# Convolved feed-forward block: four up products from unscaled rows, the other forty from normalised rows, and a later embedding product

## The chip, the cores and the metric

The kernel runs on one core of a Trainium2 chip. The metric is the device time of one execution in microseconds, the median of several runs. The engines are TensorE (PE, with its weight loads shown as PEld), VectorE (DVE), ScalarE (ACT), GpSimd (POOL) and SyncE (SP, which here only issues transfers).

## The reference, cut to what matters

One layer of a streaming encoder over 2048 positions of 1024 channels, in float32:

```python
def rms_norm(x, g):
    return x * rsqrt(mean(x * x, -1) + 1e-6) * g

h = rms_norm(x, mix_norm_g);  z = h @ w_in                # 3328 columns
y = concat(short_conv_mixer(z[:, :1536]), rwkv7_mixer(z[:, 1536:]))
x = x + y @ w_out
# feed-forward: 5632 = 2 * 2816 columns
u = causal_dwconv(rms_norm(x, ffn_norm_g) @ ffn_w_up, conv_w) + conv_b   # width 3, per channel
gate, val = split(u, 2)
x = x + (silu(gate) * val) @ ffn_w_down
# per-layer embedding
e = rms_norm(p @ ple_w_proj, ple_norm_g)
x = x + sigmoid(rms_norm(x, ple_gate_norm_g) @ ple_w_gate) * e
out = rms_norm(x, final_norm_g)
```

`causal_dwconv` at position t reads positions t-2, t-1 and t of the same channel. `rwkv7_mixer` is a recurrence over the positions.

## The kernel before, in words

**Layout.** Channels lie on the 128 partitions, positions on the free axis. The positions are cut into four groups of G = 512, so one tile is 128 x 512 and a row of 1024 channels is KD = 8 tiles. Every dense product is made in three passes of a split format: a float32 tile is held as a rounded high part `hi` and a remainder `lo`, weights as `whi`, `wlo`, and `mm3` issues whi x hi, whi x lo and wlo x hi for each of the 8 tiles, in the order of the tiles: 24 matmuls for one output tile ("a product"). Products are written to a PSUM tile of tag `d`, of which there are three.

**Stages.** First the input projection of all four groups. Then, for each group, `dense_rest`: 8 out products (`whlo` in the trace), 44 up products (`whlu`), of which numbers i and 22 + i make pair i, down products (`whld`) after every fourth pair, the embedding products (`ple_embed`, `whlpj`), and 8 gate products (`whlg`). The recurrence of the time mixer (16 units) is a generator of small steps on the side; `drive` issues one step at about every half product, so its small matmuls stand between the large ones. It has ended before the fourth group's dense work begins.

**Order.** The matmuls keep the order in which the program issues them. On the other engines a planner orders instructions when the kernel is built: among those that are ready it takes the first in program order, with all that stands in a `high_priority` block ahead of the rest. A queue then runs in that fixed order, and the first instruction that waits holds all behind it. POOL also issues the loads of the split weights (line 161); in the first group it makes them (line 154).

**The rows and their scale.** After each out product the tile `x2[m]` is squared into a running sum, and split into `hi`, `lo` of x2 times the gain (line 214 on ACT, 215 on DVE), without the factor 1/rms of the position, which needs all 8 tiles. `product` therefore starts the up products from unscaled rows: the results of the first two (HELD = 2) are copied to SBUF (line 281), then `rstd` makes the factor by one matmul (`ps_norm`) and a chain of ACT and DVE instructions (lines 239 to 248). From then on the factor is applied in each evacuation: `scaled` multiplies the PSUM tile by it into a tile `zb` with two columns in front (line 255 on DVE), POOL copies the last two columns of the previous group in and the new ones out (lines 256 and 257), ACT makes `uf` = w2 * zb + bias (line 412), and DVE adds the two shifted terms (line 417, twice). For a pair, `act_pair` then makes silu(gate) * val (lines 429 to 433) and splits it (line 153 on ACT, 154 on POOL).

**Buffers.** `hi` and `lo` tiles share 32 slots (tag `act`), working tiles of tag `b` share 6, `zb` has 2.

Of the kernel before, what the change touches and what calls it, by code (L numbers as in the profile page):

```python
# [9 lines left out]
F32 = mybir.dt.float32  # L10
F32R = mybir.dt.float32r
AF = mybir.ActivationFunctionType
ALU = mybir.AluOpType
# [3 lines left out]
P = 128  # L17
G = 512
KD = 8
FIN = 1  # L20
PLE_AT = 2
HELD = 2
WAIT = 20
R_BONUS = 1
# [13 lines left out]
NFF = 22  # L38
# [24 lines left out]
def tile_trunk(  # L63
# [18 lines left out]
    nc = tc.nc  # L82
# [13 lines left out]
    cpool = ctx.enter_context(tc.tile_pool(name="cpool", bufs=1))  # L96
# [23 lines left out]
    def v(name, i, n=1):  # L120
        o, _ = VEC[name]
        return vec[:, o + i : o + i + n]
# [19 lines left out]
    z_last = cpool.tile([P, 14], F32, tag="z_last", name="z_last")  # L142
    cx_last = cpool.tile([P, 4, 2], F32, tag="cx_last", name="cx_last")
    u_last = cpool.tile([P, 44, 2], F32, tag="u_last", name="u_last")
    for t in (z_last, cx_last, u_last):
        nc.vector.memset(t, 0.0)

# [4 lines left out]
    def residual(raw, hi, lo):  # L152
        nc.scalar.copy(hi, raw)  # L153
        nc.gpsimd.tensor_tensor(out=lo, in0=raw, in1=hi.bitcast(F32), op=ALU.subtract)  # L154

    def half(pools, src, name, key):
        t = pools["w"].tile([P, 1024], F32R, tag="whl", name=f"whl{name}", bufs=WHL)
        hi, lo = t[:, 0:512], t[:, 512:1024]
        if key in kept:
            with tc.high_priority():  # L160
                nc.gpsimd.dma_start(out=t, in_=kept[key])  # L161
            return hi, lo
        first = pools["w"].tile([P, 512], F32, tag="raw", name=f"raw{name}", bufs=WRAW)
        with tc.high_priority():
            if len(src.shape) == 3:
                nc.sync.dma_start(out=first.rearrange("p (j c) -> p j c", j=2), in_=src)
            else:
                nc.sync.dma_start(out=first, in_=src)
            residual(first, hi, lo)
        keep = dram.tile([P, 1024], F32, tag=f"k{name}", name=f"k{name}")  # L170
        nc.sync.dma_start(out=keep, in_=t.bitcast(F32))
        kept[key] = keep
        return hi, lo
# [3 lines left out]
    def weight(pools, src, name):  # L177
        return [
            half(pools, src[:, 512 * c : 512 * c + 512], f"{name}_{c}", f"{name}_{c}")
            for c in range(2)  # L180
        ]
# [5 lines left out]
    def mm3(ps, w, k, h, start, stop):  # L187
        whi, wlo = w[k // 4]
        cols = blk(k % 4)
        hhi, hlo = h  # L190
        matmul(ps, whi[:, cols], hhi, start=start, stop=False)
        matmul(ps, whi[:, cols], hlo, start=False, stop=False)
        matmul(ps, wlo[:, cols], hhi, start=False, stop=stop)
# [4 lines left out]
    def buf(pools, name):  # L198
        return pools["tmp"].tile([P, G], F32, tag="b", name=name, bufs=NBUF)
# [6 lines left out]
    def slot(pools, name):  # L206
        return pools["act"].tile([P, G], F32R, tag="act", name=name)

    def pair(pools):
        return slot(pools, "hi"), slot(pools, "lo")  # L210
# [42 lines left out]
    def scaled(pools, ps, rstd, halo, pad):  # L253
        zb = pools["tmp"].tile([P, G + 2], F32, tag="zb", name="zb")
        nc.vector.tensor_tensor(out=zb[:, 2 : G + 2], in0=ps, in1=rstd, op=ALU.mult)  # L255
        nc.gpsimd.tensor_copy(zb[:, 2 - pad : 2], halo)
        nc.gpsimd.tensor_copy(halo, zb[:, G + 2 - pad : G + 2])
        return zb
# [10 lines left out]
    def product(pools, w, rows, evac):  # L269
        ps = pools["psd"].tile([P, G], F32, tag="d", name="ps_mm")  # L270
        for k in range(KD):
            mm3(ps, w, k, rows.hs[k], k == 0, k == KD - 1)
            if k == 3:
                yield
        if rows.ss is None or rows.scale is not None:
            with tc.high_priority():
                evac(ps, rows.scale)
        else:
            with tc.high_priority():
                raw = buf(pools, "raw")  # L280
                nc.scalar.copy(raw, ps)
            rows.held.append((raw, evac))
            if len(rows.held) == HELD:
                rows.scale = rows.ss.rstd(pools)
                with tc.high_priority():
                    for raw, evac in rows.held:
                        evac(raw, rows.scale)
        yield
# [59 lines left out]
    def ple_rows(pools, g):  # L348
        hs = []
        with tc.high_priority():  # L350
            for k in range(2):
                hi, lo = pair(pools)
                t = staged(pools, pT[k, :, g * G : (g + 1) * G], "p")
                residual(t, hi, lo)
                hs.append((hi, lo))
        return hs

    def ple_embed(pools, g, st):
        hs = st
        ss = SumSq()  # L360
        for mp in range(KD // 2):
            w = quad(pools, w_proj, mp, f"pj{mp}")
            for mm in range(2):
                m = 2 * mp + mm
                ps = pools["psd"].tile([P, G], F32, tag="d", name="ps_e")
                for k in range(2):
                    mm3(ps, w, 2 * k + mm, hs[k], k == 0, k == 1)
                with tc.high_priority():
                    t = buf(pools, "e")
                    nc.scalar.copy(t, ps)  # L370
                    nc.scalar.dma_start(out=es[g][:, m, :], in_=t)
                ss.add(pools, t)
            yield
        embed[g] = ss
# [12 lines left out]
    def dense_rest(pools, g, yrows, nxt):  # L387
        tmp = pools["tmp"]
        gs = slice(g * G, (g + 1) * G)
        x2 = []  # L390
        rows = Rows()
# [13 lines left out]
            if m == FIN and pending:  # L405
                pending.pop()()

        def up(n, st, key):
            def evac(ps, rstd):
                zb = scaled(pools, ps, rstd, u_last[:, n, :], 2)  # L410
                u = st[key] = buf(pools, "uf")
                nc.scalar.activation(  # L412
                    u, zb[:, 2 : G + 2], AF.Identity,
                    bias=v("ffn_conv_b", n), scale=v("ffn_conv_w", 88 + n),
                )
                for d in (1, 0):
                    nc.vector.scalar_tensor_tensor(  # L417
                        out=u, in0=zb[:, d : d + G], scalar=v("ffn_conv_w", 44 * d + n),
                        in1=u, op0=ALU.mult, op1=ALU.add,
                    )  # L420
            return product(pools, weight(pools, w_up[n], f"u{n}"), rows, evac)

        def act_pair(i, acts):
            st = {}
            yield from up(i, st, "g")
            yield from up(NFF + i, st, "v")
            with tc.high_priority():
                th = buf(pools, "th")
                nc.scalar.activation(th, st["g"], AF.Tanh, scale=0.5)
                nc.vector.scalar_tensor_tensor(  # L430
                    out=th, in0=th, scalar=1.0, in1=st["g"], op0=ALU.add, op1=ALU.mult
                )
                nc.vector.tensor_tensor(out=th, in0=th, in1=st["v"], op=ALU.mult)
                hi, lo = pair(pools)
                residual(th, hi, lo)
                acts.append((hi, lo))
# [3 lines left out]
        def down(first, acts, last=False):  # L440
            n = len(acts) // 2
            for mp in range(KD // 2):
# [18 lines left out]
                        yield  # L461
                yield

        prev = None
        for first in range(0, NFF, NB):
            acts = []
            for i in range(first, min(first + NB, NFF)):
                if i == first + 2 and prev is not None:
                    yield from down(first - NB, prev)
                yield from act_pair(i, acts)  # L470
                if i == PLE_AT - 1:
                    prows = ple_rows(pools, g)
                if i == PLE_AT:
                    yield from ple_embed(pools, g, prows)
                if i == PLE_AT + 1:
                    embed[g] = embed[g].rstd(pools)
# [7 lines left out]
        for m in range(KD):  # L484
            nxt(m)
            w = weight(pools, w_gate[m], f"g{m}")
# [4 lines left out]
            def evac(ps, rstd, m=m, e=e):  # L491
                th = buf(pools, "gt")
                nc.vector.tensor_tensor(out=th, in0=ps, in1=rstd, op=ALU.mult)
                if m:
                    ss.add(pools, x2[m - 1])
                nc.scalar.activation(th, th, AF.Tanh, scale=0.5)
                nc.vector.scalar_tensor_tensor(
                    out=th, in0=th, scalar=1.0, in1=e, op0=ALU.add, op1=ALU.mult
                )
                nc.vector.scalar_tensor_tensor(  # L500
                    out=x2[m], in0=th, scalar=pg_h[:, m : m + 1], in1=x2[m],
                    op0=ALU.mult, op1=ALU.add,
                )
                if m == KD - 1:
                    ss.add(pools, x2[m])
# [428 lines left out]
    pools, rp = {}, {}  # L934
# [24 lines left out]
    rows = {(kind, g): Rows() for kind in ("in", "out") for g in range(NG)}  # L959
# [114 lines left out]
```

## Time and profile before

| what | value |
|---|---|
| median of 3 runs | 2914.36 us (2904.48 to 2923.4) |
| the profiled execution's own time | 2908.45 us |
| its span, first to last instruction | 2906.5 us |
| mean granted clock of TensorE | 0.984 of full speed |
| busy: PE, DVE, POOL, ACT | 95%, 66%, 38%, 33% of the span |

A stretch of the trace is given in microseconds from the start of the span. The up products of the four groups run at 747 to 1230, 1350 to 1804, 1912 to 2366 and 2465 to 2840, with the down and embedding products among them. Consecutive matmuls overlap in the record, so their spacing, not their mean duration, tells the rate.

### The profile page before, as it was taken

How to read it: one execution, taken by the hardware profiler on the slowest of the kernel's cores; microseconds unless marked ns; L12 is line 12 of the kernel's file. 1: busy time of each engine (PE TensorE's matmuls, PEld its weight loads, DVE VectorE, ACT ScalarE, POOL GpSimd, SP SyncE). 2: the span in 40 equal slices, each digit the busy share in tenths (PEclk: the TensorE clock that was granted, in tenths of full speed). 3: DMA queues.
4: the chain of work that ended last, by engine and by line, in shares of the span. 5: the costliest groups of instructions: out<-in, count | busy, mean ns of one | idle time of the engine just before them, and what ended most of it. 6: DMA issues, size and time to landing. Idle time of an engine off the chain costs nothing.

```text
span 2906.5 us, 42153 instructions
## 1 busy us (share of the span) xinstructions
PE 2768.1 (95%) x15464; PEld 2226.7 (77%) x15464; DVE 1908.3 (66%) x3039; ACT 959.9 (33%) x1721; POOL 1117.4 (38%) x1700
## 2 busy tenths in 40 slices
PE   8999999999889999989999999999999999999997
PEld 5778888778677877767778887777788877788885
DVE  5575665648587868796766676857676765544446
ACT  5332232312553433443412223434222143411113
POOL 4533232324556565652333333333333332433221
PEclk9999999999999999989999999999999999999998
DMA  8887777767777777767666565766565668666665
GB/s 298 297 261 217 236 214 223 209 210 243 263 252 245 258 241 247 248 228 230 178 186 185 173 192 172 233 202 200 174 192 169 187 187 266 216 195 189 196 188 169
DMA packets 285802, 629.95 MB, mean 217 GB/s; under 512 B 60186, under 2 KB 113690, under 8 KB 285596
## 3 DMA queue, kind: packets, MB, share of 16 engines
q0 software_dynamic: 95040, 346.07, 39.4%
q1 hardware_dynamic: 134144, 232.83, 24.0%
q10 hardware_dynamic: 56412, 48.36, 5.2%
q8 instruction: 122, 2.00, 0.3%
q14 instruction: 84, 0.69, 0.1%
HBM read 467.77 MB, written 159.38 MB: 216 GB/s over the span
## 4 chain that ended last, share of the span: by engine, by line
PE 50%; DVE 22%; DMA 14%; issue 6%; ACT 5%; POOL 3%; ACTq 1%; SPq 0%; DVEq 0%; POOLq 0%
PE ps_mm L86 33%; PE ps_d L86 11%; DVE uf L417 3%; DVE pd L794 3%; DVE xs L798 2%; DMA lm<-ld 1%; DMA xd<-xs 1%; DMA ld<-ltt 1%; DVE zb L255 1%; DVE sq L229 1%; DMA es<-e 1%; PE o_ps L86 1%; DMA dt<-xd 1%; DVE lo L215 1%; DMA x<-in_xT 1%
## 5 line engine op out<-in xcount | busy, mean ns | idle before, releaser
L86 PE MATMUL ps_mm<-hi,whlu 128*128 128x512 f32 x2816 | 910.6, 397 | 11.3 <-POOL whlu L154 5.1
L86 PEld LDWEIGHTS ps_mm<-hi,whlu 128*128 128x128 f32 x2816 | 532.3, 189 | 131.9 <-POOL whlu L154 7.8
L86 PE MATMUL ps_mm<-hi,whlin 128*128 128x512 f32 x1664 | 542.9, 400 | 19.6 <-ACT whlin L153 7.1
L86 PE MATMUL ps_mm<-lo,whlu 128*128 128x512 f32 x1408 | 552.3, 392 | 1.5 <-DVE lo L215 1.5
L86 PE MATMUL ps_d<-hi,whld 128*128 128x512 f32 x1408 | 456.1, 396 | 16.7 <-DMA whld<-kd 7.2
L86 PEld LDWEIGHTS ps_mm<-hi,whlin 128*128 128x128 f32 x1664 | 316.7, 190 | 93.0 <-ACT whlin L153 7.1
L417 DVE SCALAR_TENSOR_TENSOR uf<-zb,vec,uf 128x512 f32<-128x512 f32 x352 | 298.6, 851 | 89.6 <-ACT uf L412 78.4
L86 PE MATMUL ps_mm<-lo,whlin 128*128 128x512 f32 x832 | 328.9, 395 | 2.8 <-DVE lo L215 2.8
L412 ACT ACTIVATE uf<-zb,vec 128x512 f32<-128x512 f32 x176 | 143.1, 815 | 562.0 <-DVE zb L255 536.8
L86 PEld LDWEIGHTS ps_d<-hi,whld 128*128 128x128 f32 x1408 | 265.6, 189 | 79.2 <-DVE x L457 8.4
L86 PEld LDWEIGHTS ps_mm<-lo,whlu 128*128 128x128 f32 x1408 | 266.8, 189 | 56.2 <-DVE lo L215 2.4
L161 POOL DMA_DIRECT2D whlu<-ku x264 | 141.7, 537 | 436.8 <-PE ps_mm L86 289.1
L255 DVE TENSOR_TENSOR zb<-ps_mm,rstd 128x512 f32<-128x512 f32 x216 | 148.5, 688 | 208.0 <-PE ps_mm L86 204.4
L86 PE MATMUL ps_d<-lo,whld 128*128 128x512 f32 x704 | 275.4, 391 | 0.0
L457 DVE TENSOR_TENSOR x<-ps_d,x 128x512 f32<-128x512 f32 x192 | 131.6, 687 | 139.5 <-PE ps_d L86 138.7
L86 PEld LDWEIGHTS ps_mm<-lo,whlin 128*128 128x128 f32 x832 | 158.4, 190 | 38.1 <-DVE lo L215 6.6
L161 POOL DMA_DIRECT2D whlin<-kin x156 | 84.1, 539 | 248.9 <-PE ps_mm L86 207.7
L86 PE MATMUL ps_mm<-hi,whlg 128*128 128x512 f32 x512 | 169.2, 406 | 3.4 <-DMA whlg<-kg 3.4
L86 PE MATMUL ps_mm<-hi,whlo 128*128 128x512 f32 x512 | 163.1, 397 | 8.5 <-DMA whlo<-ko 4.9
L154 POOL TENSOR_TENSOR lo<-th,hi 128x512 fp32r<-128x512 f32 x88 | 115.2, 1310 | 110.9 <-ACT hi L153 110.3
L154 POOL TENSOR_TENSOR whlu<-rawu,whlu 128x512 fp32r<-128x512 f32 x88 | 122.6, 1398 | 88.9 <-ACT whlu L153 79.2
L86 PEld LDWEIGHTS ps_d<-lo,whld 128*128 128x128 f32 x704 | 133.2, 189 | 26.0
(205 smaller groups left out, 4248.0 us busy)
## 6 DMA issues: line engine op xcount, KB each, us to landing
whlu<-ku POOLq DMA_DIRECT2D x264, 512.0 KB, 4.5
whlin<-kin POOLq DMA_DIRECT2D x156, 512.0 KB, 4.8
whld<-kd POOLq DMA_DIRECT2D x132, 512.0 KB, 4.0
ku<-whlu SPq DMA_DIRECT2D x88, 512.0 KB, 4.7
kin<-whlin SPq DMA_DIRECT2D x52, 512.0 KB, 5.3
whlo<-ko POOLq DMA_DIRECT2D x48, 512.0 KB, 5.5
whlg<-kg POOLq DMA_DIRECT2D x48, 512.0 KB, 3.9
rawu<-in_w_up SPq DMA_DIRECT2D x88, 256.0 KB, 4.1
```

Source lines behind the costliest of these rows:

```text
L86: return pin(nc.tensor.matmul(*args, **kw))
L154: nc.gpsimd.tensor_tensor(out=lo, in0=raw, in1=hi.bitcast(F32), op=ALU.subtract)
L161: nc.gpsimd.dma_start(out=t, in_=kept[key])
L215: nc.vector.scalar_tensor_tensor(out=lo, in0=src, scalar=gcol, in1=hi.bitcast(F32), op0=ALU.mult, op1=ALU.subtract)
L229: nc.vector.tensor_tensor(out=sq, in0=sq, in1=self.acc, op=ALU.add)
L255: nc.vector.tensor_tensor(out=zb[:, 2 : G + 2], in0=ps, in1=rstd, op=ALU.mult)
L412: nc.scalar.activation(u, zb[:, 2 : G + 2], AF.Identity, bias=v("ffn_conv_b", n), scale=v("ffn_conv_w", 88 + n),)
L417: nc.vector.scalar_tensor_tensor(out=u, in0=zb[:, d : d + G], scalar=v("ffn_conv_w", 44 * d + n), in1=u, op0=ALU.mult, op1=ALU.add,)
L457: nc.vector.tensor_tensor(out=x2[m], in0=ps, in1=x2[m], op=ALU.add)
L794: tt(out=pd[:, :, :, 0:n], in0=xs[:, :, None, 0:n].broadcast_to([P, 8, 2, n]), in1=lm[:, None, i : i + 2, 0:n].broadcast_to([P, 8, 2, n]), ...
L798: nc.vector.tensor_reduce(out=xs[:, :, i : i + 2], in_=pd[:, :, :, 0:n], op=ALU.add, axis=mybir.AxisListType.X,)
```

## The change

The first four up products of a group (pairs 0 and 1) are computed and evacuated as before. While they run, `norm_rows` makes the eight rows anew with the factor applied, as a second set of `hi`, `lo`: three rows after pair 0's second product, three after pair 1's first, two after its second. The other 40 products take these rows, so that their PSUM tile is already scaled: ACT and DVE read it directly, without `zb`. The two columns that reach back into the previous group are made once for all 44 products (`halos`) and added to the first two columns. ACT, not POOL, keeps the last two columns. The embedding's rows, products and factor move back by two pairs (`PLE_AT` from 2 to 4).

```diff
-PLE_AT = 2
+PLE_AT = 4
+RAW_UP = 2
...
+    halo = cpool.tile([P, 44, 2], F32, tag="halo", name="halo")
...
+        nrows = Rows()
+        nrows.ss = None
+
+        def halos():
+            w0, w1 = v("ffn_conv_w", 0, 44), v("ffn_conv_w", 44, 44)
+            tt = nc.vector.tensor_tensor
+            tt(out=halo[:, :, 1], in0=u_last[:, :, 0], in1=w0, op=ALU.mult)
+            tt(out=halo[:, :, 0], in0=u_last[:, :, 1], in1=w1, op=ALU.mult)
+            tt(out=halo[:, :, 0], in0=halo[:, :, 0], in1=halo[:, :, 1], op=ALU.add)
+            tt(out=halo[:, :, 1], in0=u_last[:, :, 1], in1=w0, op=ALU.mult)
+
+        def norm_rows(a, b):
+            with tc.high_priority():
+                for k in range(a, b):
+                    xn = buf(pools, "xn")
+                    nc.vector.scalar_tensor_tensor(
+                        out=xn, in0=x2[k], scalar=v("ffn_norm_g", k), in1=rows.scale,
+                        op0=ALU.mult, op1=ALU.mult,
+                    )
+                    hi, lo = pair(pools)
+                    nc.scalar.copy(hi, xn)
+                    eng = nc.gpsimd if k % 2 else nc.vector
+                    eng.tensor_tensor(out=lo, in0=xn, in1=hi.bitcast(F32), op=ALU.subtract)
+                    nrows.hs.append((hi, lo))
+
-        def up(n, st, key):
-            def evac(ps, rstd):
+        def up(n, st, key, normed):
+            def evac_raw(ps, rstd):
                 zb = scaled(pools, ps, rstd, u_last[:, n, :], 2)
...
-            return product(pools, weight(pools, w_up[n], f"u{n}"), rows, evac)
+
+            def evac(ps, _):
+                u = st[key] = buf(pools, "uf")
+                nc.scalar.activation(
+                    u, ps, AF.Identity,
+                    bias=v("ffn_conv_b", n), scale=v("ffn_conv_w", 88 + n),
+                )
+                nc.scalar.copy(u_last[:, n, :], ps[:, G - 2 : G])
+                nc.vector.tensor_tensor(
+                    out=u[:, 0:2], in0=u[:, 0:2], in1=halo[:, n, :], op=ALU.add
+                )
+                for d in (1, 2):
+                    nc.vector.scalar_tensor_tensor(
+                        out=u[:, d:G], in0=ps[:, 0 : G - d],
+                        scalar=v("ffn_conv_w", 88 - 44 * d + n), in1=u[:, d:G],
+                        op0=ALU.mult, op1=ALU.add,
+                    )
+
+            w = weight(pools, w_up[n], f"u{n}")
+            return product(pools, w, nrows if normed else rows, evac if normed else evac_raw)
 
         def act_pair(i, acts):
             st = {}
-            yield from up(i, st, "g")
-            yield from up(NFF + i, st, "v")
+            yield from up(i, st, "g", i >= RAW_UP)
+            if i == 1:
+                norm_rows(3, 6)
+            yield from up(NFF + i, st, "v", i >= RAW_UP)
+            if i == 0:
+                norm_rows(0, 3)
+            if i == 1:
+                norm_rows(6, KD)
...
+        halos()
         prev = None
```

## Rows read from the trace of the kernel before

**Rows 1.** Page, busy time of each engine, its share of the span, and instructions.
```profile
PE 2768.1 (95%) x15464; PEld 2226.7 (77%) x15464; DVE 1908.3 (66%) x3039; ACT 959.9 (33%) x1721; POOL 1117.4 (38%) x1700
```
**Rows 2.** Windows, up stages: stretch, length, busy (count) PE PEld DVE ACT POOL, clock, DMA.
```profile
747.50:1229.60 482.10, 450.76 (x2788) 357.86 (x2786) 364.37 (x525) 211.35 (x392) 283.24 (x286) 0.99 0.72 249
1349.60:1804.20 454.60, 442.98 (x2778) 356.19 (x2776) 307.93 (x529) 135.01 (x254) 161.60 (x290) 0.99 0.61 181
1911.90:2366.10 454.20, 440.89 (x2778) 355.19 (x2776) 307.21 (x528) 134.48 (x251) 160.36 (x289) 0.99 0.60 179
2464.60:2840.20 375.60, 372.99 (x1638) 306.91 (x1637) 173.19 (x249) 89.81 (x132) 121.14 (x247) 1.00 0.67 199
```
**Rows 3.** Waits of PE at 787 to 1229: total us, times, longest.
```profile
PE ps_mm L86 <- POOL whlu L154: 5.1, 6, 1.4
PE ps_d L86 <- DVE x L457: 4.0, 3, 1.7
PE ps_g L86 <- DVE suv L655: 3.5, 2, 2.8
PE ps_b L86 <- ACT tok L757: 3.5, 1, 3.5
```
**Rows 4.** Waits of PE, first at 1391 to 1804, then 1956 to 2366.
```profile
PE ps_g L86 <- DVE suv L655: 2.8, 2, 2.5
...
PE ps_g L86 <- DVE suv L655: 3.1, 1, 3.1
```
**Rows 5.** Chain of waits, fourth group: start, us, what.
```profile
2633.60 43.52 PE ps_mm L86 x192
```
**Rows 6.** Groups by line at 2640 to 2830: busy, mean ns | idle before.
```profile
L417 DVE SCALAR_TENSOR_TENSOR uf<-zb,vec,uf 128x512 f32<-128x512 f32 x48 | 36.0, 751 | 24.7 <-ACT uf L412 24.3
...
L255 DVE TENSOR_TENSOR zb<-ps_mm,rstd 128x512 f32<-128x512 f32 x23 | 15.9, 693 | 44.8 <-PE ps_mm L86 44.8
L154 POOL TENSOR_TENSOR lo<-th,hi 128x512 fp32r<-128x512 f32 x12 | 15.5, 1292 | 15.7 <-ACT hi L153 15.7
...
L153 ACT CAST hi<-th 128x512 fp32r<-128x512 f32 x12 | 7.5, 622 | 30.4 <-DVE th L433 30.4
```
**Rows 7.** Groups by line, first at 747 to 1230, the last row at 1350 to 2366.
```profile
L417 DVE SCALAR_TENSOR_TENSOR uf<-zb,vec,uf 128x512 f32<-128x512 f32 x88 | 93.2, 1062 | 16.6 <-ACT uf L412 15.1 <-issue 0.4 <-POOL whlu L154 0.2
...
L257 POOL COPY u_last<-zb 128x2 f32<-128x2 f32 x44 | 21.0, 477 | 16.6 <-DVE zb L255 16.5
...
L635 ACT COPY nrd<-ksum 64x4 f32<-64x4 f32 x28 | 5.4, 192 | 13.7 <-DVE ksum L631 13.4
```
**Rows 8.** Timeline, fourth group, PE, then DVE: start, us, instruction, count, idle before.
```profile
2475.49 1.02 PE L86 MATMUL ps_norm<-sq,ones 128*128 128x512 f32 x2
...
2482.37 1.29 DVE L255 TENSOR_TENSOR zb<-raw,rstd 128x512 f32<-128x512 f32 x2
...
2494.06 0.69 DVE L255 TENSOR_TENSOR zb<-ps_mm,rstd 128x512 f32<-128x512 f32 x1
```
**Rows 9.** Timeline of DVE, third group.
```profile
1935.92 1.29 DVE L255 TENSOR_TENSOR zb<-raw,rstd 128x512 f32<-128x512 f32 x2
...
1950.03 0.69 DVE L433 TENSOR_TENSOR th<-th,uf 128x512 f32<-128x512 f32 x1
...
1954.69 0.69 DVE L255 TENSOR_TENSOR zb<-ps_mm,rstd 128x512 f32<-128x512 f32 x1 [2.15 <-PE ps_mm L86]
```
**Rows 10.** Timeline of DVE, first group.
```profile
769.66 1.29 DVE L255 TENSOR_TENSOR zb<-raw,rstd 128x512 f32<-128x512 f32 x2
...
789.81 0.69 DVE L255 TENSOR_TENSOR zb<-ps_mm,rstd 128x512 f32<-128x512 f32 x1
```
**Rows 11.** Timeline of PE, third group, start of the up products.
```profile
1919.93 0.50 PE L86 MATMUL ps_mm<-hi,whlu 128*128 128x512 f32 x1 [3.12 <-ACT hi L214]
```
**Rows 12.** Windows, the ten microseconds after that wait, columns as in Rows 2.
```profile
1920.00:1930.00 10.00, 9.71 (x63) 6.91 (x63) 0.67 (x1) 2.06 (x5) 1.55 (x3) 0.83 0.74 239
```

## The prediction

> **What bounds the kernel now.** I read the busy times first. TensorE is busy for 95% of the span and VectorE for 66% [rows 1], so a change that relieves VectorE and GpSimd pays only where TensorE waits for them. The windows of the four up stages say how much that can be: TensorE is idle there for 31.3, 11.7, 13.3 and 2.6 us [rows 2], 59 us in all, 2% of the span. The waits of TensorE say what ends these gaps once the first products are over: in the first group weight remainders on GpSimd (5.1), down results that VectorE has not yet added (4.0), and two kinds of wait of the time mixer (3.5 each) [rows 3]; in the second and third mainly the mixer's wait for VectorE, 2.8 and 3.1 [rows 4]. That is 22 us which a lighter VectorE and GpSimd could shorten. In the fourth group, without mixer work, the chain shows 192 matmuls in 43.52 us [rows 5]: 0.227 us each, 5.44 us a product, with nothing between them. There the change can win almost nothing.
>
> Below, p1 to p5 are the first five up products of a group, and row 0 to row 7 its eight normalised rows.
>
> **What is removed.** For each of 160 products (4 groups x 40): on VectorE the scaling, 0.69 us [rows 6]; on GpSimd two copies, the one shown taking 0.48 us in the first group [rows 7], so about 38 us of its 283 us of work there [rows 2]. The shifted additions remain, but read PSUM and one SBUF tile instead of two SBUF tiles. The trace has no such instruction. Its nearest rows are 0.69 us (scaling, one PSUM input) and 0.75 us (shifted addition from SBUF, unhindered) [rows 6], while in the first group, with GpSimd busy, the same addition took 1.06 us and in the second and third less [rows 7]. I take 0.69, as the row with a PSUM input; the ends are 0.69 and 1.06. The Trainium skill, page "VectorE: DVE Perf Modes", section "Rules for kernel authors", speaks against the change: where many operations follow on a matmul's output, it advises copying PSUM to SBUF first. The rows here do not show PSUM to be dearer (0.69 against 0.75), and by the page the sum would differ only in VectorE's busy time, which is not the bound.
>
> **What is added per product.** On ACT a copy of two columns, 0.19 us by the smallest ACT copy [rows 7]; on VectorE an addition of two columns, which I put at the same 0.19. ACT's conversion keeps its length. So VectorE saves 0.69 + 2 x 0.75 - 2 x 0.69 - 0.19 = 0.62 us a product unhindered, 25 us of 173 to 308 us in a group [rows 2], and about 50 us in the first. None of it lies on TensorE's path directly; what it returns is a part of those 22 us. I take half, **11 us**; the ends are 0 and 35 (all of the listed waits, and as much again of small ones left out here, about 13).
>
> **What is added once per group: the eight rows.** Each needs a two-input VectorE instruction (0.75), an ACT cast (0.62) and a remainder, on VectorE for even rows (0.69) and on GpSimd for odd ones (1.29) [rows 6]. On VectorE that is 8 x 0.75 + 4 x 0.69 = 8.8 us. The rows can begin when the factor is there, and must be done while p3 and p4 run, which is short. In the fourth group the norm matmul starts at 2475.49 and the factor is first used at 2482.37 [rows 8]. After the norm (about 0.8 us with the restart), p3 and p4 take 10.9 us, so p5 starts at 2487.2, under 5 us after the factor, and would end at 2492.6. And VectorE has no room: from 2482.37 it runs without a gap until 2494.06, 16 instructions in 11.7 us, 0.73 us each: the evacuations of p1 to p4, all kept by the change, and the two tails of `act_pair` [rows 8]. The planner takes ready urgent work in program order, and the program puts the evacuations of p1 and p2 ahead of row 0, that of p3 ahead of row 3 and that of p4 ahead of row 6. Only the last tail (two instructions) comes after row 7. So 16 - 2 + 12 = 26 instructions at 0.73 us run from 2482.37 to 2501.4; the last remainder, on GpSimd, ends about then (cast 0.62 and 1.29 after the last row's start of work), and the last three matmuls follow: p5 ends near 2502 instead of 2492.6. **9.5 us.**
>
> In the third group the mixer's matmuls lie between the products, which gives time, and its VectorE work, which takes some back. VectorE is in use from 1935.92 to 1950.72, and p5's end is marked by its scaling at 1954.69 [rows 9]. Adding 8.8 and taking off 1.4 for the last tail gives 1958.1, and 1 us for the end of the last remainder and its matmuls 1959.1: **4.5 us**. The second group repeats these times to 0.3 us: 4.5. In the first group the same queue of 22.2 us after 769.66 ends at 791.9, with 1 us as before 792.9, against 789.81 [rows 10]; since two-input instructions took 1.06 and not 0.75 there [rows 7], I add 2: **5 us**. Together 23.5 us; the ends are 8 (rows ahead of the evacuations: at most 2 a group) and 50 (GpSimd's remainders queue behind its weight loads, which wait for TensorE).
>
> **The clock.** After a wait of 3.12 us [rows 11] the granted clock over the next 10 us was 0.83 [rows 12]: part of it at 1.2 instead of 2.4 GHz, 1.7 us of full-speed work lost. Each of the four waits for the rows is of that size or larger, and p5 is fed one row at a time. I add 4 x 1.7 = **7 us**; the ends are 0 and 14. The Trainium skill, page "TensorE: Matmul & The Clock Gate", Part 1, says that the low level is the default and that activity lifts it; the row agrees. Without that rule the sum would be 7 us less.
>
> **What is moved or costs nothing.** The embedding keeps its 48 matmuls, two loads on SP, eight stores on ACT's queue and four weight loads on POOL; moved by two pairs they stand between other up products of the same kind. The factor's chain moves to pair 5, still far ahead of the gate stage that needs it. If the cover is gone, it is the idle time that remains in the fourth group, 2.6 us [rows 2]. The four small `halos` instructions (under 0.7 us each, as a 512-column one) run during p1 and p2, when VectorE waits for the factor. The slots: 16 unscaled and 16 normalised tiles fill all 32, so row 7 and pair 0's tile wait until p4 gives slots back, which it does before VectorE gets to row 7: nothing. In the new evacuation ACT's copy and VectorE both read the PSUM tile, and the tile is held through the conversion and both additions, about 0.8 + 0.2 + 0.2 + 1.4 = 2.6 us instead of 0.7; two more tiles give 10.9 us of room, so nothing unless VectorE is far behind (second rival).
>
> **Sum.** 2908.45 + 23.5 + 7 - 11 = 2928 us on the profiled execution. The median of the runs is 6 us above that execution, so a measured median may lie at 2934; I say **2930**.
>
> **The rivals.**
> *The rows come in time.* If the planner, or the wait for `zb` (two buffers), lets the rows run ahead of the evacuations, their 8.8 us after 2483.7 end at 2492.5, and p5 is late by 2 us at most. For it: p6, not p5, is the first to need a late evacuation. Against it: program order. Then 2908 + 4 - 11 to 35 = 2877 to 2901, likely 2890.
> *PSUM is held.* VectorE in the first three groups is far enough behind that TensorE waited for its down sums (4.0 us in 3 waits, [rows 3]). Each normed product keeps its tile 1.9 us longer; where the queue is more than 10.9 us behind, every such product adds up to that. With about 12 of them 23 us come on top: 2951. It decides from the point at which waits of TensorE for `uf` appear among the up products. Against it: VectorE carries 0.6 us less per product.
> *Given back.* TensorE's delay lets weights, GpSimd and the mixer catch up, so that later waits shrink by what p5 lost; the first group has 31 us of them [rows 2]. Then the sum comes to 2908 + 30.5 - 22 - 5 = 2912.
>
> **How the numbers follow.** Within 1% is 2885 to 2943, what a measurement can tell from no change. Chances: the forecast 0.45, rows in time 0.25, PSUM held 0.13, given back 0.17. Faster by over 1% needs the better half of the first rival: 0.14. Slower by over 1% takes a third of the forecast (the rows' upper ends) and most of the second rival: 0.27. The rest, 0.59, is no change. The range runs from 2890 (rows in time) to 2960 (second rival, or 50 us for the rows with the clock); the forecast's own is 2910 to 2950.
>
> **What would show it.** Waits of TensorE for `lo` and `hi` of lines in `norm_rows`, 4 to 10 us in each group about 25 us after its up products begin; a lower granted clock right after them; the `zb` scaling down to 16 of 176 in the up products; a smaller wait for the mixer and for GpSimd in the first group. It is wrong if those waits for rows are missing, or if TensorE waits for `uf`.

## The result and the profile after

The changed kernel takes 2955.4 us (median of 3 runs, 2952.52 to 2955.84) against 2914.36: a ratio of 1.015, with a 95% interval of 1.0126 to 1.0174. It is slower by 37 to 51 us, where 16 us were forecast; the time lies inside the stated range and outside the forecast's own of 2910 to 2950. The profiled execution took 2955.84 us at a granted clock of 0.974. Its busy times, answering to [rows 1]:

```profile
PE 2783.6 (94%) x15464; PEld 2234.2 (76%) x15464; DVE 1866.6 (63%) x3103; ACT 983.1 (33%) x1913; POOL 1055.3 (36%) x1396
```

VectorE is lighter by 42 us and GpSimd by 62, and yet the span is 48 us longer. The groups by line (columns as in [rows 6]) show that the evacuation was exchanged as described: the scaling from PSUM (last line) is left 56 times in the whole span, 48 of them outside the up products; the first two lines are the new shifted addition and the addition of the two columns.

```profile
L460 DVE SCALAR_TENSOR_TENSOR uf<-ps_mm,vec,uf 128x511 f32<-128x511 f32 x320 | 238.6, 745 | 12.5 <-ACT u_last L455 2.4
L456 DVE TENSOR_TENSOR uf<-uf,halo 128x2 f32<-128x2 f32 x160 | 42.7, 267 | 206.0 <-ACT uf L451 139.0 <-ACT u_last L455 66.6
L257 DVE TENSOR_TENSOR zb<-ps_mm,rstd 128x512 f32<-128x512 f32 x56 | 38.5, 688 | 48.7 <-PE ps_mm L87 48.4
```

The windows of the four up stages, and after them of three stretches of ten microseconds in the fourth (columns as in [rows 2]):

```profile
753.80:1232.20 478.40, 449.11 (x2786) 358.86 (x2785) 341.30 (x540) 216.57 (x440) 262.82 (x210) 0.98 0.72 250
1352.10:1821.60 469.50, 449.76 (x2778) 359.13 (x2776) 300.91 (x543) 140.54 (x300) 144.91 (x214) 0.97 0.60 175
1929.20:2398.50 469.30, 445.30 (x2778) 356.11 (x2776) 300.95 (x544) 140.79 (x299) 145.13 (x213) 0.98 0.59 173
2498.40:2887.70 389.30, 377.19 (x1637) 308.85 (x1637) 165.30 (x261) 94.90 (x180) 112.73 (x171) 0.98 0.65 191
2520.00:2530.00 10.00, 3.61 (x15) 2.35 (x13) 9.96 (x15) 3.50 (x7) 5.25 (x8) 0.83 0.49 152
2530.00:2540.00 10.00, 7.32 (x16) 4.89 (x17) 9.25 (x9) 3.50 (x6) 5.97 (x5) 0.50 0.21 53
2540.00:2550.00 10.00, 10.00 (x45) 8.31 (x44) 4.71 (x8) 2.18 (x5) 3.38 (x5) 0.99 0.57 156
```

Against [rows 2] the stages are 3.7 us shorter in the first group and 14.9, 15.1 and 13.7 us longer in the others: 40 of the 48 us. Another 6.3 us lie ahead of the first up stage (753.8 against 747.5), where the change adds no work; over the traces of the experiments that start lies anywhere from 745 to 755, so this part is not put down to the change. The fourth group, which has no mixer work, shows the mechanism bare. The waits of TensorE there, at 2498 to 2560 (total, times, longest), are all for the rows:

```profile
PE ps_mm L87 <- ACT hi L430: 5.4, 1, 5.4
PE ps_mm L87 <- DVE lo L432: 2.2, 2, 1.2
PE ps_mm L87 <- POOL lo L432: 1.5, 1, 1.5
```

VectorE (first fence) and GpSimd (second) in that stretch, by the timeline (start, us, instruction, count):

```profile
2517.42 2.07 DVE L425 SCALAR_TENSOR_TENSOR xn<-x,vec,rstd 128x512 f32<-128x512 f32 x3
2519.41 2.44 DVE L444 SCALAR_TENSOR_TENSOR uf<-zb,vec,uf 128x512 f32<-128x512 f32 x2
...
2528.69 4.09 DVE L444 SCALAR_TENSOR_TENSOR uf<-zb,vec,uf 128x512 f32<-128x512 f32 x3
2532.71 1.76 DVE L425 SCALAR_TENSOR_TENSOR xn<-x,vec,rstd 128x512 f32<-128x512 f32 x1
...
2536.32 0.68 DVE L432 TENSOR_TENSOR lo<-xn,hi 128x512 fp32r<-128x512 f32 x1
```

```profile
2528.84 1.73 POOL L156 TENSOR_TENSOR lo<-th,hi 128x512 fp32r<-128x512 f32 x1 [1.96 <-ACT hi L155]
...
2530.53 3.39 POOL L432 TENSOR_TENSOR lo<-xn,hi 128x512 fp32r<-128x512 f32 x2
```

VectorE works through rows and evacuations without a gap from 2516.2 to 2537; its last remainder of a row is made at 2536.3. While GpSimd subtracts, three additions take 4.09 us and one scaling of a row 1.76, where 0.75 is the unhindered time [rows 6]. TensorE's clock is at 0.83, 0.50 and 0.99 in the three windows above: about (1 - 0.83)/0.5 x 10 + 10 = 13.4 us at the lower level, 1.2 GHz, of which about 10 follow the long wait, which ends at 2530.0.

In the second and third group the waits for rows are small. Other waits stand in the list of TensorE's waits at 1352 to 1480:

```profile
PE ps_e L87 <- POOL lo L156: 3.0, 2, 2.8
PE ps_d L87 <- DVE ms L242: 2.6, 1, 2.6
PE s_ps L87 <- DVE suv L643: 2.1, 1, 2.1
...
PE ps_mm L87 <- DVE lo L432: 1.4, 2, 1.1
```

The first is the embedding product's wait for the split input `p`, the second is a down product that waits for the embedding's factor, the third belongs to the mixer. Why `p` is late shows in the order of ACT's (first fence) and GpSimd's queue in the timeline:

```profile
1429.10 0.62 ACT L155 CAST hi<-th 128x512 fp32r<-128x512 f32 x1 [0.87 <-DVE th L485]
1429.63 0.61 ACT L776 CAST pbh<-pb 128x512 fp32r<-128x512 f32 x1
1430.15 1.14 ACT L155 CAST hi<-p 128x512 fp32r<-128x512 f32 x2
```

```profile
1429.81 1.77 POOL L156 TENSOR_TENSOR lo<-th,hi 128x512 fp32r<-128x512 f32 x1 [0.75 <-ACT hi L155]
1431.55 1.26 POOL L777 TENSOR_TENSOR pbl<-pb,pbh 128x512 fp32r<-128x512 f32 x1
1432.77 2.94 POOL L156 TENSOR_TENSOR lo<-p,hi 128x512 fp32r<-128x512 f32 x2
```

`p` was loaded at 1345 to 1350. Its two tiles are split at 1430 to 1436, behind the pair's `th` and behind `pb`, `pbh` and `pbl` of a mixer unit, while the first embedding matmul starts at 1430.8. In the kernel before, the same tiles were split at 1386.9 to 1391 for an embedding at 1397, with no wait.

### The profile page after: what moved, and what is told of

The parts are those of the page before. It is cut to its first block, busy times and chain, and to the rows that moved or that the text cites. A ratio compares the mean times of both kernels' runs of the same rounds, so it can differ in the third digit from the quotient of the medians.

```text
span 2954.1 us, 41986 instructions
## 1 busy us (share of the span) xinstructions
PE 2783.6 (94%) x15464; PEld 2234.2 (76%) x15464; DVE 1866.6 (63%) x3103; ACT 983.1 (33%) x1913; POOL 1055.3 (36%) x1396
## 5 line engine op out<-in xcount | busy, mean ns | idle before, releaser
L87 PE MATMUL ps_d<-hi,whld 128*128 128x512 f32 x1408 | 462.2, 401 | 29.8 <-DVE ms L242 9.6
L451 ACT ACTIVATE uf<-ps_mm,vec 128x512 f32<-128x512 f32 x160 | 124.6, 779 | 507.2 <-PE ps_mm L87 493.5
L460 DVE SCALAR_TENSOR_TENSOR uf<-ps_mm,vec,uf 128x511 f32<-128x511 f32 x320 | 238.6, 745 | 12.5 <-ACT u_last L455 2.4
L456 DVE TENSOR_TENSOR uf<-uf,halo 128x2 f32<-128x2 f32 x160 | 42.7, 267 | 206.0 <-ACT uf L451 139.0
L163 POOL DMA_DIRECT2D whld<-kd x132 | 71.7, 543 | 255.4 <-PE ps_d L87 153.1
```

The source lines that it names most:

```text
L87: return pin(nc.tensor.matmul(*args, **kw))
L451: nc.scalar.activation(u, ps, AF.Identity, bias=v("ffn_conv_b", n), scale=v("ffn_conv_w", 88 + n),)
L456: nc.vector.tensor_tensor(out=u[:, 0:2], in0=u[:, 0:2], in1=halo[:, n, :], op=ALU.add)
L460: nc.vector.scalar_tensor_tensor(out=u[:, d:G], in0=ps[:, 0 : G - d], scalar=v("ffn_conv_w", 88 - 44 * d + n), in1=u[:, d:G], op0=ALU.mult ...
```

## The experiments

All ratios are against the kernel before on the same chip, with 95% intervals; 0.1% is 2.9 us. Unless an edit says otherwise, it is made on the changed kernel. Differences between two experiments have a range worked out from both intervals.

**1. The embedding back at pair 2.** `PLE_AT = 2` in the changed kernel.

> The changed kernel with the embedding back at pair 2. Theory: two parts of the change cost, and they add. The late rows cost about 13 us in the fourth group and little net in the others; the embedding's new place costs about 10 us in each of the first three groups (its rows queue behind the mixer's work on POOL, and its factor's PSUM tile is still held when the down products begin). So taking the move back gives 2925 us, about 30 below the changed kernel. Rival (PSUM tiles held longer by the new evacuation are the cost): the move is worth nothing and the time stays at 2950 to 2957.

2927.75 us, 1.0092 [1.0078, 1.0106]: the theory's direction, against the rival. By the ratios the move of the embedding is worth 1.0150 - 1.0092 = 0.58%, 17 us (9 to 25 by the two intervals), about half of the theory's 30; by the bare times it is 28 us, but the kernel before took 2914.36 us beside the changed kernel and 2901.94 us beside this one. The three waits for rows in the fourth group are the same to 0.1 us.

**2. The move alone.** `PLE_AT = 4` in the kernel before.

> The kernel before with nothing but the embedding moved to pair 4. Theory: 20 to 30 us slower than before, 2934 to 2944, with waits of the embedding products for the remainders of p and of the first down products for the factor's chain in the first three groups, nothing in the fourth. Rival (held PSUM tiles, or the rows alone): no change, 2910 to 2920.

2910.37 us, 1.0035 [1.0022, 1.0048], 10 us: between theory and rival. The move costs without the rows as well, by the same waits (TensorE for `lo` of `p`: 3.8 us in the second group), but less.

**3. All rows first.** The rows are issued as soon as the factor is there, ahead of the evacuations of p1 and p2:

```diff
...
+                if rows.on_scale:
+                    rows.on_scale()
                 with tc.high_priority():
                     for raw, evac in rows.held:
...
-                norm_rows(0, 3)
...
-                norm_rows(3, 6)
...
-                norm_rows(6, KD)
...
+        rows.on_scale = lambda: norm_rows(0, KD)
```

> The changed kernel with all eight rows issued ahead of the evacuations of the first two products, embedding at pair 4. Theory: VectorE's order makes the rows late; 12 of its instructions after the factor are then the rows', the fifth product of the fourth group waits at most 2 us instead of 9 to 13, its clock stays high, and the time falls by about 15 us to 2940. Rival (the work itself is too much for the time that two products give, whatever its order): no change against 2955, since the waits move to the evacuations and from there to PSUM tiles of the products after the fifth.

2947.71 us, 1.0159 [1.0145, 1.0173]: the rival is right for the whole. The fourth group's up stage came to 381.2 us, 5.6 over [rows 2] instead of 13.7, as the theory said. The other groups lost it again. TensorE's waits in the second group, 1351 to 1480, are now for the embedding's factor and mixer tiles:

```profile
PE ps_d L87 <- DVE ms L242: 3.7, 1, 3.7
...
PE w_ps L87 <- ACT suv L642: 2.7, 1, 2.7
PE u_ps L87 <- DVE w_t L642: 2.0, 1, 2.0
```

**4. Rows first, embedding at pair 2.** Experiments 1 and 3 together.

> Both: rows ahead of the evacuations and the embedding back at pair 2. Theory of two costs that add: 2955 - 30 - 15 = 2910 us, a little under the kernel before, as what is left is the lighter VectorE and GpSimd. Rival (held PSUM tiles): 2940 or more, with waits of TensorE for the additions into uf.

2933.97 us, 1.0107 [1.0081, 1.0132]: the theory fell. Another order of the same work is not better than that of experiment 1.

**5. The evacuation alone.** `PLE_AT = 2`, no rows made, the 40 products take the unscaled rows (`nrows.hs = rows.hs`), so that the factor is left out of their results.

> Embedding at pair 2, the direct evacuation kept, but no rows are made: all 44 products take the unscaled rows, so for 40 of them the factor 1/rms is left out of the result. This prices the new evacuation alone. Theory (the rows are the cost, the lighter evacuation a gain): 5 to 15 us faster than the kernel before, most of it in the first group, the fourth equal within 1 us. Rival (PSUM tiles held longer are the cost): 5 to 15 us slower than before, with waits of the down products for VectorE in the second and third group.

2903.9 us, 0.9991 [0.9973, 1.001]: a gain of -3 to 8 us, below the 11 of the sum and between theory and rival. In its profile VectorE is busy for 1815.0 us, 93 less than before, and GpSimd 95 less; TensorE did not need it. In the first group 3.9 us in three waits of TensorE are for `uf`, a tile held by the new evacuation.

**6. The rows alone.** The kernel before (`PLE_AT = 2`, no `halos`), the rows made in pairs 0 and 1, read by no product.

```diff
-            return product(pools, w, nrows if normed else rows, evac if normed else evac_raw)
+            return product(pools, w, rows, evac_raw)
```

> The kernel before with the rows made as in the change (embedding at pair 2) but read by nobody; all products as before. This prices VectorE's work for the rows without a product that waits for them. Theory (the rows also stand ahead of the mixer's urgent copies, for which TensorE waits in its fixed order): 10 to 15 us slower than before, 3 to 5 in each of the first three groups, nothing in the fourth. Rival (only the fifth product's wait for its rows costs): within 4 us of before.

2947.75 us, 1.0148 [1.0124, 1.0172], far over what was expected. Nothing waits for the rows, and they cost as much as the whole change. TensorE's wait in the fourth group at 2530 to 2570, and then the instruction waited for on ACT:

```profile
PE ps_e L87 <- ACT hi L155: 10.8, 1, 10.8
```

```profile
2548.00 0.62 ACT L155 CAST hi<-th 128x512 fp32r<-128x512 f32 x1 [1.07 <-DVE th L485]
2548.72 0.63 ACT L481 ACTIVATE th<-uf 128x512 f32<-128x512 f32 x1
2549.26 1.12 ACT L155 CAST hi<-p 128x512 fp32r<-128x512 f32 x2
```

The embedding comes next and its `p` stands on ACT behind `th`, which waits for VectorE. VectorE's backlog is handed to what TensorE needs next.

**7. The embedding between.** `PLE_AT = 1`, so that its 48 matmuls stand between p4 and p5 and give the rows time.

> The changed kernel with the embedding at pair 1, so that its 48 matmuls (11 us of TensorE that need no row) stand between the fourth and the fifth up product. Theory (the rows are late by 9 to 10 us because two products are too short a time): the fourth group's loss of 13 us falls to 3 or less, the whole is 5 to 12 us above the kernel before instead of 26 (embedding at pair 2) or 44. Rival (the embedding's own evacuations and squares lengthen VectorE's and ACT's queues by as much): it stays 20 us or more above before.

2930.64 us, 1.007 [1.0053, 1.0087]: the rival. The rows are in time, and in the fourth group TensorE waits 8.8 us for `hi` of `p` instead. The interval overlaps experiment 1's; these two are the best of the versions whose products read the rows.

**8. The same with rows outside the priority block.** `with tc.high_priority():` in `norm_rows` replaced by `if True:`.

> The same, with the rows outside the urgent block, so that the mixer's urgent copies go ahead of them where both are ready; the order in the fourth group is the same. Theory (in the first three groups the rows hold the mixer's copies): another 5 to 10 us less than with urgent rows, at or under the kernel before. Rival (the rows are then late for the fifth product by more than the mixer gains): 5 us or more above the version with urgent rows.

2933.56 us, 1.0101 [1.0081, 1.012]: the theory fell, and the time is 0.3% above experiment 7, 9 us, as the rival has it, with intervals that just overlap.

**9. The factor of the embedding later.** `if i == PLE_AT + 2`.

> The changed kernel (embedding at pair 4) with the embedding's factor after pair 6 instead of after pair 5, so that an up product and not a down stage of short products follows it. Theory (of the 17 us that the move costs, a part is the factor's PSUM tile, which the first down products wait for): 6 to 10 us less than the changed kernel, about 1.2% above before. Rival (only the late rows of p cost): no change, 1.5% above before.

2946.68 us, 1.0134 [1.0112, 1.0157]: overlaps the changed kernel's interval, so not decided.

**10. The split of `p` earlier.** `if i == 1: prows = ple_rows(pools, g)`, the embedding's products still after pair 4.

> The changed kernel with the rows of p made right after pair 1 instead of after pair 3, ahead of the mixer's next unit on POOL; embedding still after pair 4. Theory (the other part of the move's cost is that these rows stand behind the mixer's work on ACT and POOL, about 5 us of embedding time in each of the first three groups): 8 to 14 us less than the changed kernel, about 1.1% above before. Rival (the embedding's ACT and VectorE work costs wherever its rows are made): no change.

2937.29 us, 1.0118 [1.0098, 1.0138], as the theory has it: 9 us of the move's 17, though barely clear of noise (0 to 18 by the two intervals). The tile's instructions in the second group (duration minimum/median/maximum in ns, first and last start):

```profile
L155 ACT CAST hi<-p x2: 604/612/621, 1393.9 to 1394.9; 128x512 fp32r<-128x512 f32 x2
L156 POOL TENSOR_TENSOR lo<-p,hi x2: 1300/1301/1302, 1394.6 to 1395.8; 128x512 fp32r<-128x512 f32 x2
```

Nobody waits for them now, and TensorE's busy time for the same matmuls is 2771.5 us where the changed kernel had 2783.6.

**11. Experiments 9 and 10 together.**

> Both of these edits. Theory: together they take back the whole cost of the move, so the time is that of the changed kernel with the embedding at pair 2, 0.9% (26 us) above before, or a little less. Rival: 1.3% or more, with a third cause in the new place.

2938.75 us, 1.0112 [1.0089, 1.0135]: the same as 10. The factor's place is worth nothing that these runs can show; what TensorE waits for instead stands in the next section.

**12. `p` split ahead of pair 0, embedding after pair 1.**

> Embedding after pair 1 as before, but its rows made ahead of pair 0, so that they do not stand behind the rows' queue, and its 48 matmuls can run while VectorE finishes the rows. Theory (the lost time is VectorE's backlog, and any TensorE work that needs nothing of that queue hides it): about 0.3 to 0.5% above before instead of 0.7 to 1.0%. Rival (the copies of the embedding products on ACT stand behind the same queue, and three PSUM tiles are all the room): 0.7% or more.

2933.71 us, 1.0104 [1.0086, 1.0123]: the rival. In the fourth group TensorE now waits 8.2 us for the embedding's own evacuation on ACT (`e`, line 372), behind the same queue.

**13. The rows alone, spread.** Experiment 6 with one row after each product of pairs 2 to 5.

```diff
-            if i == 1:
-                norm_rows(3, 6)
+            if 2 <= i <= 5:
+                norm_rows(2 * i - 4, 2 * i - 3)
...
+            if 2 <= i <= 5:
+                norm_rows(2 * i - 3, 2 * i - 2)
```

> The kernel before with the eight rows made and read by nobody, as in the run that cost 1.48%, but one row after each product of pairs 2 to 5 instead of all eight within pairs 0 and 1. The same VectorE, ScalarE and GpSimd work is done. Theory (the place: VectorE is full only in the 12 us after the factor, and the same 8.8 us of work elsewhere is covered): 0 to 6 us slower than before, 1.000 to 1.002. Rival (the amount: VectorE hands on every microsecond wherever it is put): 30 to 42 us slower, 1.010 to 1.015.

2916.75 us, 1.0047 [1.003, 1.0064]: more than the theory's 1.002, and far under the rival. The same work costs 14 us instead of 43. The fourth group's window:

```profile
2469.40:2845.70 376.30, 373.45 (x1637) 306.54 (x1636) 186.44 (x261) 93.45 (x140) 129.18 (x251) 1.00 0.65 198
```

VectorE is as busy as in experiment 6 (186.4 against 186.6 us in the stage); the stage is 0.7 us longer than before instead of 12.4. No product reads these rows: a kernel that makes them so late and reads them needs more products from unscaled rows, and was not run.

**14. The rows alone, without GpSimd's part.** Experiment 6 with the four remainders of odd rows left out.

```diff
-                    eng = nc.gpsimd if k % 2 else nc.vector
-                    eng.tensor_tensor(out=lo, in0=xn, in1=hi.bitcast(F32), op=ALU.subtract)
+                    if k % 2 == 0:
+                        nc.vector.tensor_tensor(out=lo, in0=xn, in1=hi.bitcast(F32), op=ALU.subtract)
```

> The kernel before with the eight rows made in pairs 0 and 1 and read by nobody, with the four remainders of GpSimd left out (a row read by nobody needs none). VectorE has as many instructions as in the run that cost 1.48%. Theory (contention: VectorE's three-operand instructions take twice as long beside GpSimd's remainders, some 4 to 6 us a group, 16 to 24 in all): 1.007 to 1.010. Rival (the number of instructions alone fills VectorE): 1.012 to 1.015.

2933.63 us, 1.0105 [1.0084, 1.0125], between the two, nearer to the theory: about 0.4%, 12 us, with intervals that just touch. VectorE's row instructions, groups by line, first of experiment 6 and then of this one:

```profile
L425 DVE SCALAR_TENSOR_TENSOR xn<-x,vec,rstd 128x512 f32<-128x512 f32 x32 | 26.0, 844 | 0.1
...
L432 DVE TENSOR_TENSOR lo<-xn,hi 128x512 fp32r<-128x512 f32 x16 | 15.2, 952 | 0.0
```

```profile
L425 DVE SCALAR_TENSOR_TENSOR xn<-x,vec,rstd 128x512 f32<-128x512 f32 x32 | 22.9, 752 | 0.1
...
L432 DVE TENSOR_TENSOR lo<-xn,hi 128x512 fp32r<-128x512 f32 x16 | 11.9, 746 | 0.0
```

**15. The new evacuation with rows that nobody reads.** Experiment 5 with the rows made in pairs 0 and 1.

> The new evacuation for the other 40 products with unscaled rows (their factor is left out, as in the run without rows), embedding at pair 2, and the eight rows made in pairs 0 and 1 but read by nobody. Beside the run without rows it adds only the making of the rows; beside the run of the change with the embedding at pair 2 (0.92% slower than before) it takes away only the products' wait for them. Theory (the backlog costs, not the wait; the lighter evacuation gives back some 15 to 20 us of it, because it empties the queue sooner): 1.006 to 1.010. Rival (the wait for the rows is the cost and the dead rows cost 42 us only with the heavy evacuation's stage behind them): under 1.004. Second rival (the lighter evacuation gives nothing here either): 1.013 or more.

2938.68 us, 1.0113 [1.0091, 1.0136], just over the theory's 1.010; the interval reaches into the second rival as well. Against experiment 1 (1.0092), whose products do wait for the rows, it is no faster: no cost of the wait beside the backlog shows. Against experiment 6 (1.0148) the new evacuation gives back about 0.35%, 10 us, with overlapping intervals.

## Why the prediction was wrong in size

**The moved embedding: the step that failed.** The prediction priced it at nothing, because "moved by two pairs they stand between other up products of the same kind". The matmuls do. The split of `p` did not come along unharmed: it moved on ACT and GpSimd behind a pair's `th` and a mixer unit, which the fourth pair falls together with. Measured: 17 us beside the rows (experiment 1), and 10 without them (2). The waits of TensorE in the whole span of the changed kernel show where they go:

```profile
PE ps_e L87 <- POOL lo L156: 9.0, 5, 2.8
PE ps_e L87 <- ACT hi L155: 3.4, 3, 1.4
PE ps_d L87 <- DVE ms L242: 9.6, 4, 5.4
PE ps_d L87 <- DVE x L509: 9.2, 6, 2.7
```

In experiment 1 the first three (the split of `p`, and the embedding's factor) are not there, and the fourth (VectorE's down sums) is

```profile
PE ps_d L87 <- DVE x L509: 12.8, 8, 2.7
```

That is 12.4 us of waits for `p` and 18.8 - 12.8 = 6 for the factor and the sums: 18 us, about the 17. Splitting `p` earlier takes away the first part and gives back 9 of the 17 (10). Of the other 8 (0 to 15 by the intervals of 10 and 1) the second part is what the traces show. A later factor does not gain it: in experiment 11 no product waits for the factor, and the waits for the sums come to 15.9 us, with no gain in time that shows.

**Rows and relief together: +19.5 forecast, +27 measured** (0.92%, 23 to 31, experiment 1). With the 17 us above these are the 24 us that the sum lacked: 1.5% of 2908 is 44, the sum had 19.5.

**The relief is not a term of its own.** Taken alone it is -3 to 8 us (5), not 11: VectorE lost 93 us of work there (25 us a group and 50 in the first, as predicted, are 125; the two-column addition took 267 ns, not 190), and of the 22 us of waits in [rows 3, 4] that the sum halved, no gain that can be measured came. Where the rows have filled VectorE it is about 10, not clear of noise (6 against 15). Correspondingly the rows cost 43 us with the old evacuation and 29 with the new (0.9991 to 1.0092), against 30.5 in the sum with the clock. The two edits share VectorE's queue and do not simply add up: 43 - 3 = 40 us against the 27 of both together (1), a difference of 4 to 23 by the three intervals.

**The rows: place right, mechanism too narrow.** The fourth group went nearly as worked out from [rows 8]: 9.1 us of waits against 9.5, and 13.7 us with the clock against 11.2. The order was not quite the one worked out: three rows went ahead of the additions of p1 and p2 (2517.42). In the other groups TensorE waits only some 2 to 3 us for rows at p5, not 4.5 to 5; other waits of the mixer and of the embedding appear there (3). Where no product reads the rows, the next thing that TensorE needs from the far end of VectorE's queue pays in the reader's place, with waits of 10.8 and 8.7 us (6, 15). Neither order (3, 4, 8) nor cover (7, 12) removed the cost; putting the work elsewhere took away 29 of 43 us (13).

**GpSimd beside VectorE.** The prediction took 0.73 us an instruction and kept a surplus for the first group only [rows 7]. Experiment 14 shows what GpSimd's remainders add: 844 against 752 ns for a scaling, 952 against 746 for a remainder. The Trainium skill, "SBUF — State Buffer", section "Who interferes with whom", says that a VectorE instruction with two SBUF inputs contends with a GpSimd instruction that reads SBUF; experiment 14 agrees, and the new additions, which read PSUM for one input, kept a mean of 745 ns.

**The clock.** 1.7 us a group was too little for the fourth: there TensorE's busy time for the same matmuls rose from 372.99 to 377.19 us, by 4.2. The clock was at 1.2 GHz for 13.4 us, while p5 was fed in pieces. In the whole span the busy time rose by 15.5 us (2768.1 to 2783.6) where the sum had 7. It rose by 4.5 in experiment 1, by 0.8 in experiment 2 and by 16.5 in experiment 6 (2772.6, 2768.9 and 2784.6), so it cannot be put down to one part of the change.

**The rivals.** Rows in time: not in the changed kernel, and without a gain clear of noise where more nearly brought about (3 against the changed kernel, 7 against 1). PSUM held: TensorE waits for no `uf` in the changed kernel, and 3.9 us in experiment 5, which is no slower than before; nothing near 23 us. Given back: the first group's stage shortened by 3.7 us; in the second and third the new waits outweighed whatever came back. The rule on copying PSUM to SBUF first, which the prediction cites from the Trainium skill ("VectorE: DVE Perf Modes", "Rules for kernel authors"), did not decide: additions from PSUM took 745 ns against 751 unhindered from SBUF [rows 6].

No version with rows beats the kernel before, and the new evacuation without them gained at most about 8 us.

## What to carry to other kernels

An engine that is 66% busy over the span can be full for the 12 us in which new work is due; count what stands in its queue there, and measure what the same work costs elsewhere (43 us against 14 here). Test a relief by itself before adding it to a sum: it is worth something only where the relieved engine is what the bound one waits for. When a step moves, list its preparations on every queue and what they now stand behind; its matmuls are the smaller part.

## What was not expected of the hardware

Beside subtractions on GpSimd, VectorE's instructions with two SBUF inputs took up to 1.76 us instead of about 0.75. The subtractions took longer too: GpSimd's own remainder of a pair 1.73 us at 2528.84 instead of 1.29 [rows 6]. And TensorE stayed at the lower clock level for about 10 us after a wait of 5.4 us, with two more of 1.5 and 1.2 in them, against 3.4 us after the single wait of 3.12 us in [rows 11, 12].
